# The passages into and out of W_up in a hybrid encoder layer: split order, product order, and the order of loads, sums and stores

## The chip, the cores and the metric

The kernel runs on one core of a Trainium2 chip. The core has five engines with an instruction stream each: PE (matrix products, with PEld for its weight loads), DVE (VectorE), ACT (ScalarE), POOL (GpSimd) and SP (SyncE, which here issues every DMA). They wait for each other through semaphores. The metric is the device time of one execution in microseconds (us); lower is better. Three runs of the kernel before took 1406.53, 1408.93 and 1409.12 us, median 1408.93.

## The reference

One layer of a streaming encoder on 1024 prompt rows and 64 sample rows of width 1024: an input projection, three kinds of mixing (forgetting attention, a gated unit, stick-breaking attention), an output projection, a layer norm, and then the part that matters here:

```
def sq_relu_mlp(x, w_up, w_down):
    h = jnp.square(jax.nn.relu(jnp.einsum('btd,df->btf', x, w_up)))
    return jnp.einsum('btf,fd->btd', h, w_down)

xp = layer_norm(ALPHA * xp + sq_relu_mlp(xp, w_up[l], w_down[l]), ln2_g[l], ln2_b[l])
```

W_up is 1024 by 4096 and W_down 4096 by 1024, all in float32; the sample rows go through the same layer.

## The kernel before, in words

Every float32 product is made from three passes in a faster format: each operand is split into a high part (a copy by ScalarE) and a low part (a subtraction, line 97, by VectorE or POOL), and high times high, high times low and low times high are added up. In place of 8 block products of a 2 by 2 blocking, the kernel computes 7 (a Strassen-like scheme), which needs sums and differences of the operands beforehand and of the results behind.

**W_up ("up", from about 690 to 1040 us).** The columns of W_up are taken in 16 pairs p of 256 columns. The rows are two token groups: s=0 with 288 columns of the products (the samples' 32 among them) and s=1 with 256. `Chain(p, s)` (L1253) holds one pair and one group: `product(i)` (L1260) is 12 matmuls at L1272 into PSUM banks named zA to zD, each followed by an evacuation (a ScalarE copy L1283 for A, VectorE sums L1286 to L1292); `relu` (L1304) makes the squared relu of the eight results in place, `sums` (L1313 to L1316) the four combinations that W_down's 7 products want, and stores them to DRAM: `h4_dr` (L1317), `h3_dr` (L1318) and for s=0 the sample columns `hs_dr` (L1321). The weights of a pair arrive by `up_load` (L1463), tile wr, are split into wa (L1212 and L97) and summed and split into ws.

The token operand comes from rows that a layer norm has just finished. `x_steps` (L1140) is a generator: for the rows of pair nm ("0" and "1" are s=0, "2" and "3" are s=1) it transposes four blocks on PE into PSUM tiles xtb, xta, xtd and xtc (tag pt, two buffers, so that the third transposition waits for what reads the first), copies and splits them into the operands xo, and forms the four combinations tt[0] to tt[3] (L1168, L1172, then L1174 or L1181, then L1182) with splits of their own. Between its steps the first products are issued by hand.

**W_down ("down", from about 1040 us on).** W_down is taken in 16 groups g of 256 of its rows, two (c = g // 2) sharing a set of split weights wd; group g multiplies the h of pairs p. `wd_load` (L1386) brings weights into rd (for the second half of the first set: into awa, the buffer that held the last wa), `wd_sum` (L1404) and `wd_split` form and split the combinations. `h_load` (L1421) reads stored h back (into hx, hr and awa), `h_split` makes its high part on ScalarE (L1431), copies that to a PSUM tile st (L1435) and subtracts on VectorE (L1436). The first h of group 0, tile h4a, is loaded by four DMAs (L1628). `Down.product` (L1730) is 6 matmuls and `evac` adds the result to accumulators (L1695, L1697), which `acc_load` (L1447, L1450) first fills with the layer's input. `first_group` (L1852) does group 0 by hand; `hs_load` and `b12_again` (L1849) belong to the samples' product (L1774, L1776), which comes behind group 0.

**What sets the order.** SP issues DMAs in program order, and each waits for the eighth before it. Inside `in_order(...)` (L99) each engine's stream is pinned to the order in which the code is written; that holds for the first up pair, the borders p=1 and from p=14, and `first_group`. Only the pairs between and the later groups are placed by the scheduler. In the last part of up, c2 is pair 14 with s=0, c3 is pair 15 with s=1, and c4 is pair 15 with s=0; c0 and c1 at the start are the first pair's chains.

Of the kernel before, what the change touches and what calls it, by code (L numbers as in the profile page):

```python
# [12 lines left out]
F32 = mybir.dt.float32  # L13
# [7 lines left out]
P = 128  # L21
PASSES = ((0, 0), (0, 1), (1, 0))
D = 1024
# [4 lines left out]
NB = TP // P  # L28
# [28 lines left out]
def _build(nc, tc, a, es):  # L57
# [1082 lines left out]
    def x_steps(nm, s, c0, n, r0, n0, r1, n1):  # L1140
# [32 lines left out]
        if s == 0:  # L1173
            nc.vector.tensor_tensor(tt[:, 2], p22, c12, op=ALU.subtract)  # L1174
# [3 lines left out]
        if s == 1:  # L1178

            split_t(4, nc.vector)  # L1180
            nc.vector.tensor_tensor(tt[:, 2], p22, c12, op=ALU.subtract)  # L1181
        nc.vector.tensor_tensor(tt[:, 3], tt[:, 1], p21, op=ALU.subtract)  # L1182
        yield
        if s == 0:
            hi = xo0[:, 3:7, :, 0, cs]
            nc.scalar.activation(hi.rearrange("p o k c -> p (o k) c"), tt.rearrange("p o k c -> p (o k) c"), AF.Copy)
            lo_sub(nc.vector, xo0[:, 3:7, :, 1, cs].rearrange("p o k c -> p (o k) c"),
                   tt.rearrange("p o k c -> p (o k) c"), hi.rearrange("p o k c -> p (o k) c"))
        else:
            for o in (3, 5, 6):  # L1190
                split_t(o, nc.vector if o < 5 or nm == "3" else nc.gpsimd)
# [132 lines left out]
    for i in range(MIXED, NT):  # L1324
        t = ORD[i]
# [132 lines left out]
    with p3:  # L1458
# [51 lines left out]
        t = ORD[-1]  # L1510
        next(x2)
        with in_order(border):
# [39 lines left out]
            low()  # L1552
            c0.finish()
            c1.product(6)
# [44 lines left out]
        def products(c, some):  # L1599
            for i in some:  # L1600
                c.product(i, False)

        with in_order(border):
# [19 lines left out]

            h4 = lp.tile([P, 2, 2, 2, 4, P], F32R, name="h4a", tag="ws")
            hbuf[0, 0], hbuf[0, 1] = h4[:, 0], h4[:, 1]
            for q in range(2):
                for x in range(2):
                    nc.sync.dma_start(h4[:, x, 1, q].bitcast(F32), h4_dr[q, 0][:, :, x * P:(x + 1) * P])  # L1628
            awa = lp.tile([P, 3, D], F32, name="awa", tag="wa")
            hx = lp.tile([P, D], F32, name="hx", tag="hx")  # L1630
# [4 lines left out]
            h_load(0, 1, 0)  # L1635
            wd_load(0, 1, awa[:, 0:2].rearrange("p q (o c) -> p (q o) c", o=2))
            products(c3, (1,))
            c2.relu()
            products(c3, (2,))
            c2.sums()  # L1640
            acc_load(0)
            products(c3, (3, 4))
            h_split(0, 0, 0, ("o", "s"))
            products(c3, (5, 6))
            c4 = chain(NP - 1, 0)
# [6 lines left out]
            def both_pairs(n):  # L1652
                for q in range(2):
                    wd_split(0, q, n, nc.gpsimd)

            both_pairs(0)
            products(c4, (1,))
            h_split(0, 0, 1, ("o", "s"))
            both_pairs(2)
            for q in range(2):  # L1660
                wd_sum(0, q, 0, nc.vector)
            products(c4, (2,))
            both_pairs(1)
            wd_sum(0, 0, 1, nc.vector)
            products(c4, (3, 4))
            wd_sum(0, 1, 1, nc.vector)
            products(c4, (5,))
            h_load(0, 1, 1)
            for q in range(2):
                wd_sum(0, q, 2, nc.vector)  # L1670
            h_split(0, 1, 0, ("tr", "s"))
            both_pairs(3)
            products(c4, (6,))
            both_pairs(4)
    xst.close()


    with ExitStack() as p3:
# [173 lines left out]
        def first_group():  # L1852
# [10 lines left out]
            for q in range(2):  # L1863
                wd_sum(0, q, 3, nc.vector)
# [5 lines left out]
            both(1)  # L1870
            for q in range(2):
                wd_split(0, q, 6, nc.gpsimd)
            for q in range(2):
                h_load(1, 1, q)
            both(2)
            h_split(1, 0, 0, None, (0,))
            c4.relu()
# [3 lines left out]
            c3.relu()  # L1881
            both(4)
            h_split(1, 0, 0, None, (1,))
            c3.sums(nc.gpsimd)
            c4.sums()
            h_split(1, 0, 1)
            both(5)
            a37 = lp.tile([P, 2, D], F32, name="acc37", tag="hh1")
            two(3, a37[:, 0])
            two(7, a37[:, 1])  # L1890
            for t in (2, 6, 3, 7, NB):
                acc_load(t)
# [15 lines left out]
        for c in range(NC - 1):  # L1908
            for part in range(2):
# [3 lines left out]
                if g == 1:  # L1913
                    hs_load(0)
                    for q in range(2):
                        b12_again(0, q)
# [191 lines left out]
```

## Time and profile before

| what | value |
|---|---|
| median of three runs | 1408.93 us |
| profiled execution, own time | 1403.64 us |
| its span, first to last instruction | 1401.8 us |
| mean granted TensorE clock | 0.984 |
| PE busy | 1323.6 us, 94% |
| VectorE, ScalarE, POOL busy | 996.3, 720.1, 608.5 us |
| DMA traffic | 168.87 MB, mean 120 GB/s |

Times in the timelines are microseconds from the span's start. A row gives start, duration, engine, line, operation, output<-inputs and count; the bracket at its end holds how long the engine had been idle before it and whose instruction released it. In rows of windows each engine has its busy time and, in round brackets, its number of instructions; the granted clock is 1.00 at full speed. SPq rows are the issue of a DMA, not its transfer; the DMA view gives the time from issue to landing.

### The profile page before, as it was taken

The numbers are of one execution on the slowest core, as the hardware profiler recorded it, in microseconds if no ns is written. First come the engines' busy times: TensorE is split into PE (matmuls) and PEld (weight loads), VectorE is DVE, ScalarE is ACT, GpSimd is POOL, SyncE is SP. The second block draws the span as 40 slices with busy tenths as digits, with TensorE's granted clock in tenths as the row PEclk, the third lists the DMA queues.
The fourth block names the chain that finished last, engine by engine and source line by source line (L and its number), as shares of the span: only waits on it lengthen the run. The fifth ranks groups of instructions, "written<-read, shape, count | busy, mean of one in ns | idle before, by whom it ended". The sixth has DMA issues, their size and how long they took to land.

```text
span 1401.8 us, 24289 instructions
## 1 busy us (share of the span) xinstructions
PE 1323.6 (94%) x8827; PEld 1205.5 (86%) x8827; DVE 996.3 (71%) x1795; ACT 720.1 (51%) x1561; POOL 608.5 (43%) x667
## 2 busy tenths in 40 slices
PE   7899999999989997999899999999998999999996
PEld 6899999999888986866789999999986788887874
DVE  3566566677787499787776677687668677667677
ACT  3366565666565476333432332322256677667665
POOL 3222232356565445755421222122156765555647
PEclk9999999999999998999999999999999999999998
DMA  7334242321313434432223444443468244344343
GB/s 219 72 84 113 58 113 66 83 59 49 95 27 80 115 97 130 143 112 68 76 85 113 160 152 131 153 141 127 162 223 316 90 169 138 130 153 146 106 135 128
DMA packets 150257, 168.87 MB, mean 120 GB/s; under 512 B 27116, under 2 KB 116524, under 8 KB 150136
## 3 DMA queue, kind: packets, MB, share of 16 engines
q1 hardware_dynamic: 150136, 167.30, 38.1%
q8 instruction: 70, 1.15, 0.3%
q14 instruction: 51, 0.42, 0.1%
HBM read 109.26 MB, written 51.71 MB: 115 GB/s over the span
## 4 chain that ended last, share of the span: by engine, by line
PE 54%; DVE 13%; DMA 10%; POOL 8%; ACT 8%; issue 5%; SPq 1%; DVEq 0%; ACTq 0%; POOLq 0%
PE zA L1272 9%; PE zD L1272 6%; PE mx L244 5%; PE kvsb L355 5%; PE kvfox L355 4%; POOL wd L97 3%; DMA rd<-w_down 3%; PE zC L1272 3%; PE zB L1272 3%; DMA awa<-h_dr 2%; POOL rd L1404 2%; PE qfox L496 2%; PE Sfox L554 2%; ACT wd L1212 2%; PE ptfox L602 1%
## 5 line engine op out<-in xcount | busy, mean ns | idle before, releaser
L97 POOL TENSOR_TENSOR wa<-wr,wa 128x512 fp32r<-128x512 f32 x42 | 63.6, 1544 | 225.3 <-ACT wa L1212 203.8
L97 POOL TENSOR_TENSOR wd<-rd,wd 128x512 fp32r<-128x512 f32 x77 | 100.5, 1317 | 108.0 <-ACT wd L1212 94.8
L244 PE MATMUL mx<-xT,oTb 128*128 128x512 f32 (+1 forms) x416 | 105.6, 405 | 1.6 <-ACT oTb L202 1.5
L1272 PE MATMUL zD<-xo,ws 128*128 128x288 f32 (+1 forms) x720 | 98.1, 289 | 3.1 <-DVE h4a L1436 2.7
L1272 PE MATMUL zA<-xo,ws 128*128 128x288 f32 (+1 forms) x720 | 98.2, 290 | 0.0
L1272 PEld LDWEIGHTS zD<-xo,ws 128*128 128x128 f32 x720 | 93.7, 189 | 3.6 <-DVE h4a L1436 2.9
L244 PEld LDWEIGHTS mx<-xT,oTb 128*128 128x128 f32 (+1 forms) x416 | 76.3, 189 | 21.1 <-ACT oTb L202 2.5
L1272 PEld LDWEIGHTS zA<-xo,ws 128*128 128x128 f32 x720 | 94.3, 190 | 0.0
L355 PE MATMUL kvfox<-wkvfox,xT 128*128 128x256 f32 (+3 forms) x624 | 90.8, 294 | 2.4 <-DVE fx L458 1.3
L540 POOL TENSOR_TENSOR sgsb<-sgsb,snsb 128x127 f32<-128x127 f32 (+7 forms) x48 | 58.9, 1228 | 78.7 <-DVE snsb L538 64.3
L1404 POOL TENSOR_TENSOR rd<-rd 128x512 f32<-128x512 f32 x56 | 79.4, 1419 | 30.4 <-DVE b L97 28.1
L355 PE MATMUL kvsb<-wkvsb,xT 128*128 128x256 f32 (+1 forms) x624 | 87.7, 286 | 0.0
L1212 ACT ACTIVATE wd<-rd 128x512 fp32r<-128x512 f32 x105 | 63.4, 623 | 44.2 <-POOL rd L1404 21.9
L1730 PE MATMUL A<-wd,wd 128*128 128x512 f32 x312 | 83.3, 396 | 3.0 <-DVE acc L1697 2.0
L355 PEld LDWEIGHTS kvfox<-wkvfox,xT 128*128 128x128 f32 (+1 forms) x624 | 81.9, 194 | 4.1 <-DVE fx L458 1.6
L538 DVE TENSOR_TENSOR_SCAN snsb<-snsb,one 128x128 f32<-128x128 f32 (+7 forms) x48 | 72.3, 1509 | 13.3 <-ACT snsb L537 12.7
L355 PEld LDWEIGHTS kvsb<-wkvsb,xT 128*128 128x128 f32 (+1 forms) x624 | 79.3, 187 | 0.2
L1283 ACT ACTIVATE sn<-zA 128x256 f32<-128x256 f32 (+1 forms) x80 | 31.0, 390 | 92.2 <-PE zA L1272 77.5
L1730 PEld LDWEIGHTS A<-wd,wd 128*128 128x128 f32 x312 | 58.0, 188 | 19.1 <-DVE acc L1697 3.5
L1730 PE MATMUL A<-wd,h4a 128*128 128x512 f32 x240 | 64.2, 393 | 1.2 <-DVE acc L1697 0.7
L1490 ACT ACTIVATE ws<-wr 128x1024 fp32r<-128x1024 f32 x28 | 29.0, 1057 | 56.9 <-DVE wr L1222 56.9
L1730 PEld LDWEIGHTS A<-wd,h4a 128*128 128x128 f32 x240 | 44.8, 188 | 12.3 <-ACT wd L1212 1.1
(548 smaller groups left out, 3750.5 us busy)
## 6 DMA issues: line engine op xcount, KB each, us to landing
h_dr<-hh SPq DMA_DIRECT2D x30, 512.0 KB, 3.2
rd<-w_down SPq DMA_DIRECT2D x30, 512.0 KB, 4.4
wr<-w_up SPq DMA_DIRECT2D x13, 1024.0 KB, 5.5
hr<-h_dr SPq DMA_DIRECT2D x31, 384.0 KB, 3.8
h_dr<-hh SPq DMA_DIRECT2D x30, 384.0 KB, 4.0
raw<-w_in SPq DMA_DIRECT2D x44, 256.0 KB, 3.4
hx<-h_dr SPq DMA_DIRECT2D x15, 512.0 KB, 3.8
awa<-h_dr SPq DMA_DIRECT2D x15, 512.0 KB, 4.1
```

The source lines that it names most:

```text
L97: eng.tensor_tensor(out, src, hi.bitcast(F32), op=ALU.subtract)
L244: nc.tensor.matmul(acc[0:m], oT[:, k, hx, 0:m], wo[k // 4][hw][:, k % 4, cs], start=(i == 0), stop=(i == len(seq) - 1))
L355: nc.tensor.matmul(acc[0:n, c0:c0 + n1 - n0], xT[k // 4][:, k % 4, c:c + n], wt[:, k, hw, n0:n1], start=(i == 0), stop=(i == len(seq) - 1))
L496: nc.tensor.matmul(acc[:, 0:w], wq[:, k, hw, :], xT[k // 4][:, k % 4, c:c + w], start=(i == 0), stop=(i == len(seq) - 1))
L538: nc.vector.tensor_tensor_scan(g[:, 0:n][:, ::-1], g[:, 0:n][:, ::-1], one.broadcast_to([P, n]), 1.0, op0=ALU.mult, op1=ALU.bypass)
L540: nc.gpsimd.tensor_tensor(s[:, 0:n - 1], s[:, 0:n - 1], g[:, 1:n], op=ALU.mult)
L1212: nc.scalar.activation(hi, raw, AF.Copy)
L1272: nc.tensor.matmul(z, w[:, hw, k], xop(s, bo, hx)[:, k, :], start=(new and k == 0 and j == 0), stop=(k == 3 and j == 2), skip_group_check= ...
L1283: nc.scalar.activation(c, z, AF.Copy)
L1404: eng.tensor_tensor(r[:, o], r[:, x], r[:, y], op=ALU.subtract)
L1490: nc.scalar.activation(ws[:, 0, q, c], src[:, q], AF.Copy)
L1730: nc.tensor.matmul(z, h[:, hx, q, o], wset[self.c % 2][q][:, hw, wb], start=((n in (0, 3) or n == 1 and self.c == 0) and q == 0 and j == 0 ...
```

## The change

It touches four places and removes no arithmetic. (1) In `x_steps` the early split of operand 4 and the late tt[2] now happen only for pair "3"; pair "2" forms tt[2] at L1174, and splits operand 4 at the end. (2) In the first pair, c1's last product comes ahead of `c0.finish()`, so c1's evacuation, relu, sums and stores stand ahead of c0's on VectorE and SP. (3) In the last pair of up, c2's relu, sums and stores come ahead of the load of W_down's second half into awa; both h_splits of h4a come ahead of c3's products 1 and 3; the loads of hx and the second h3 piece, the accumulator load and wd's sums change place; c3's relu and sums (on VectorE instead of POOL) move up from `first_group`, wd's fourth sum to the end of up. (4) In `first_group`, c4's relu and sums, the accumulator loads of tiles 3, 7 (buffer hh1) and 2, 6 (hh0) move up, and hs_load and b12_again come in from group 1.

```diff
@@ x_steps
         nc.vector.tensor_tensor(tt[:, 1], p22, tt[:, 0], op=ALU.subtract)
-        if s == 0:
+        if nm != "3":
             nc.vector.tensor_tensor(tt[:, 2], p22, c12, op=ALU.subtract)
         yield
         p21 = tr(r0, 1, n0, "c")
         both(1, p21)
-        if s == 1:
+        if nm == "3":
 
             split_t(4, nc.vector)
             nc.vector.tensor_tensor(tt[:, 2], p22, c12, op=ALU.subtract)
...
-            for o in (3, 5, 6):
+            for o in (3, 5, 6) if nm == "3" else (4, 3, 5, 6):
                 split_t(o, nc.vector if o < 5 or nm == "3" else nc.gpsimd)
@@ first pair
             low()
+            c1.product(6)
             c0.finish()
-            c1.product(6)
@@ last pair of up
                     nc.sync.dma_start(h4[:, x, 1, q].bitcast(F32), h4_dr[q, 0][:, :, x * P:(x + 1) * P])
+            hx = lp.tile([P, D], F32, name="hx", tag="hx")
+            h_load(0, 1, 0)
             awa = lp.tile([P, 3, D], F32, name="awa", tag="wa")
-            hx = lp.tile([P, D], F32, name="hx", tag="hx")
...
-            h_load(0, 1, 0)
+            c2.relu()
+            c2.sums()
             wd_load(0, 1, awa[:, 0:2].rearrange("p q (o c) -> p (q o) c", o=2))
-            products(c3, (1,))
-            c2.relu()
-            products(c3, (2,))
-            c2.sums()
+            h_split(0, 0, 0, ("o", "s"))
+            products(c3, (1, 2))
+            h_split(0, 0, 1, ("o", "s"))
+            products(c3, (3, 4))
             acc_load(0)
-            products(c3, (3, 4))
-            h_split(0, 0, 0, ("o", "s"))
             products(c3, (5, 6))
+            h_load(0, 1, 1)
             c4 = chain(NP - 1, 0)
             products(c4, (0,))
...
             both_pairs(0)
+            c3.relu()
+            c3.sums()
             products(c4, (1,))
-            h_split(0, 0, 1, ("o", "s"))
             both_pairs(2)
+            products(c4, (2,))
+            both_pairs(1)
             for q in range(2):
                 wd_sum(0, q, 0, nc.vector)
-            products(c4, (2,))
-            both_pairs(1)
-            wd_sum(0, 0, 1, nc.vector)
             products(c4, (3, 4))
-            wd_sum(0, 1, 1, nc.vector)
+            h_split(0, 1, 0, ("tr", "s"))
+            for q in range(2):
+                wd_sum(0, q, 1, nc.vector)
             products(c4, (5,))
-            h_load(0, 1, 1)
             for q in range(2):
                 wd_sum(0, q, 2, nc.vector)
-            h_split(0, 1, 0, ("tr", "s"))
             both_pairs(3)
             products(c4, (6,))
             both_pairs(4)
+            for q in range(2):
+                wd_sum(0, q, 3, nc.vector)
@@ first_group
-            for q in range(2):
-                wd_sum(0, q, 3, nc.vector)
             both(0)
...
             both(1)
+            c4.relu()
...
             both(2)
+            c4.sums()
             h_split(1, 0, 0, None, (0,))
-            c4.relu()
+            a37 = lp.tile([P, 2, D], F32, name="acc37", tag="hh1")
+            two(3, a37[:, 0])
+            two(7, a37[:, 1])
+            for t in (3, 7):
+                acc_load(t)
             both(3)
             h_load(1, 0, 1)
             wd_load(1, 0)
-            c3.relu()
+            for t in (2, 6, NB):
+                acc_load(t)
             both(4)
             h_split(1, 0, 0, None, (1,))
-            c3.sums(nc.gpsimd)
-            c4.sums()
             h_split(1, 0, 1)
+            hs_load(0)
+            for q in range(2):
+                b12_again(0, q)
             both(5)
-            a37 = lp.tile([P, 2, D], F32, name="acc37", tag="hh1")
-            two(3, a37[:, 0])
-            two(7, a37[:, 1])
-            for t in (2, 6, 3, 7, NB):
-                acc_load(t)
@@ the loop over groups
-                if g == 1:
-                    hs_load(0)
-                    for q in range(2):
-                        b12_again(0, q)
                 wd_load(c + 1, part)
```

## The prediction

> **What bounds the kernel now.** The page first, then the windows, then engine by engine the timelines of two stretches, the start of W_up (685 to 735 us) and the passage into W_down (1014 to 1090 us), because the diff touches nothing else.
>
> ```profile
> span 1401.8 us, 24289 instructions
> PE 1323.6 (94%) x8827; PEld 1205.5 (86%) x8827; DVE 996.3 (71%) x1795; ACT 720.1 (51%) x1561; POOL 608.5 (43%) x667
> ```
>
> TensorE is busy 94% of the span, and no product is added or removed. All the change can move is PE's idle time at the two borders, plus the time its clock is down. PE's timeline at the first border (start, duration, instruction, and in brackets idle time and releaser):
>
> ```profile
> 694.69 1.02 PE L1148 MATMUL xtb<-ident,y 128*128 128x128 f32 x4 [3.36 <-DVE xr L1181]
> 695.36 3.10 PE L1272 MATMUL zA<-xo,oTb 128*128 128x288 f32 x12
> ...
> 698.66 1.84 PE L1272 MATMUL zC<-xo,w 128*128 128x288 f32 x12
> 701.00 0.63 PE L1148 MATMUL xtd<-ident,y 128*128 128x128 f32 x4 [0.50 <-DVE xr L1168]
> ...
> 730.57 0.40 PE L1272 MATMUL zA<-xo,wa 128*128 128x288 f32 x1 [1.18 <-ACT wa L1212]
> 731.93 2.71 PE L1272 MATMUL zA<-xo,wa 128*128 128x288 f32 x11 [0.96 <-POOL wa L97]
> ```
>
> And at the second border:
>
> ```profile
> 1021.87 1.59 PE L1272 MATMUL zA<-xo,ws 128*128 128x256 f32 x12
> ...
> 1033.73 1.88 PE L1272 MATMUL zD<-xo,ws 128*128 128x288 f32 x12 [2.67 <-DVE h4a L1436]
> ...
> 1039.25 1.89 PE L1272 MATMUL zD<-xo,ws 128*128 128x288 f32 x12 [0.46 <-DVE hh L1286]
> 1040.97 2.89 PE L1730 MATMUL A<-wd,h4a 128*128 128x512 f32 x12
> ...
> 1064.04 1.67 PE L1730 MATMUL D<-wd,h4b 128*128 128x512 f32 x6
> ...
> 1073.46 0.98 PE L1730 MATMUL A<-wd 128*128 128x512 f32 x3 [0.87 <-DVE acc L1695]
> ...
> 1075.88 0.94 PE L1730 MATMUL A<-wd,h4a 128*128 128x512 f32 x3 [0.74 <-DVE acc L1697]
> 1077.86 0.96 PE L1730 MATMUL D<-wd 128*128 128x512 f32 x3 [1.04 <-DVE acc L1695]
> ...
> 1080.25 0.96 PE L1730 MATMUL A<-wd,wd 128*128 128x512 f32 x3 [0.75 <-DVE acc L1695]
> ...
> 1087.24 0.40 PE L1774 MATMUL ds<-wd,hs 128*128 128x512 f32 x1
> ```
>
> The brackets are the prize: 3.36, 0.50 and 2.14 us at the first border, 2.67, 0.46 and 3.40 (0.87, 0.74, 1.04 and 0.75) at the second. Some of it also costs clock. The first window follows the 2.14 us of waits at W_up's first new weights; the second holds the 2.67 us gap. After the busy times of PE, PEld, DVE, ACT and POOL the row has the granted clock:
>
> ```profile
> 733.00:735.00 2.00, 2.00 (x10) 2.00 (x10) 1.97 (x2) 0.27 (x1) 2.00 (x2) 0.50 0.00 0
> 1030.00:1040.00 10.00, 6.88 (x50) 6.41 (x49) 7.37 (x9) 6.36 (x13) 7.40 (x6) 1.00 0.18 68
> ```
>
> **First border, x_steps.** For pair "2", L1174's subtraction goes ahead, so xtd's PSUM buffer is free without waiting for L1181, and the early split of operand 4 goes to the end. VectorE's rows:
>
> ```profile
> 689.80 2.38 DVE L150 TENSOR_TENSOR y<-y,gb 128x512 f32<-128x512 f32 x2 [1.25 <-POOL y L143]
> ...
> 693.86 0.68 DVE L1181 TENSOR_TENSOR xr<-xtd,c 128x512 f32<-128x512 f32 x1
> ```
>
> The subtraction (0.68) fits into the 1.25 idle ahead of L150. So xtb starts when L150's first half is done, about 691.2, and the 3.36 goes; so does the slow clock behind it (3.10 against 1.84, 1.02 against 0.6: 1.6 in all) and the 0.50. In their place come PE's waits for the next late things, estimated from the order of the rows: about 0.6 for xta (L1182), 0.8 for zC (ScalarE's copy) and 0.5 for xtd. 3.36 + 1.6 + 0.5 - 1.9 = 3.6 us earlier at the products behind.
>
> **First border, the last product ahead of the sums.** This reorders VectorE and SP: the s=1 chain's evacuation, sums and two stores come first, the s=0 chain's with its three hs stores last, right before the load of the next weights.
>
> ```profile
> 720.30 1.28 DVE L1304 SCALAR_TENSOR_TENSOR y<-y 128x512 f32<-128x512 f32 x2
> ...
> 723.21 0.45 DVE L1288 TENSOR_TENSOR hh<-zB,sn 128x288 f32<-128x288 f32 x1
> ```
> ```profile
> 720.65 2.31 SPq L1321 DMA_DIRECT2D hs_dr<-h  x3
> ...
> 724.08 1.77 SPq L1463 DMA_DIRECT2D wr<-w_up  x2
> ```
>
> VectorE's total is unchanged, so the sums still end near 723.4. But now 2.31 us of hs stores stand between their end and the load: 726.4 instead of 724.08, and 3.6 earlier by the step above: the load is 1.3 us earlier in all. PE stands 3.6 earlier, so its wait at 730.57 grows by 2.3, and the border gains **1.3 us**. Bounds: a gain of 3.6 if the load's wait has cover that I don't see, a loss of 1.0 if the longer gap costs as much clock again as the 2.71 row (11 matmuls at 1.84/12 each would be 1.69).
>
> **Second border, h_split of the first group ahead of c3's products.** ScalarE's rows:
>
> ```profile
> 1020.66 0.39 ACT L1283 ACTIVATE sn<-zA 128x256 f32<-128x256 f32 x1 [2.41 <-PE zA L1272]
> ...
> 1023.78 0.62 ACT L1431 ACTIVATE h4a<-h4a 128x512 fp32r<-128x512 f32 x1
> 1024.43 0.60 ACT L1435 ACTIVATE st<-h4a 128x512 f32<-128x512 f32 x1
> ```
> ```profile
> 1016.44 2.79 SPq L1628 DMA_DIRECT2D h4a<-h_dr  x4
> ...
> 1053.41 0.33 SPq L1421 DMA_DIRECT2D awa<-h_dr  x1
> ...
> 1059.84 0.33 SPq L1317 DMA_DIRECT2D h_dr<-hh  x1
> ```
> ```profile
> h4a<-h_dr SPq DMA_DIRECT2D x2, 256.0 KB, 4.0
> ```
> ```profile
> h4a<-h_dr SPq DMA_DIRECT2D x2, 256.0 KB, 6.1
> ```
>
> The first two of the four h4a loads took 4.0 us to land, the last two 6.1. The third is issued near 1017.8 and lands near 1023.9. In the changed order four ScalarE instructions that need loads one and three stand ahead of the 0.39 us copy at 1020.66, which frees zA for the product that began at 1021.87. ScalarE does the last two (0.62 + 0.60) from 1023.9, then the copy: about 1025.5, and PE waits **3.6 us** where it waited for nothing. Had the third load taken 4.0, it would be 1.5. Against this the 2.67 and the 0.46 go. The 2.67 was VectorE's: its L1288 waited on the hs store, which now is ahead of the 1 MB of awa loads:
>
> ```profile
> 1032.63 0.46 DVE L1288 TENSOR_TENSOR hh<-zB,sn 128x288 f32<-128x288 f32 x1 [5.02 <-DMA hs_dr<-hh]
> ```
>
> With 0.2 of small waits W_down starts 0.7 later than 1040.97 (3.6 + 0.2 - 2.67 - 0.46). If no load blocks ScalarE it is 3.1 earlier; if the gap costs the clock, another 1.0 to 1.6 later. W_down's second half behind the h stores costs nothing itself: its first sums start at 1034 and later.
>
> **Second border, the sums and the h loads of the first groups.** The third set of wd sums now stands behind h_split(0,1,0), some 3 us later on VectorE and POOL, and hx comes free later:
>
> ```profile
> 1046.52 0.55 DVE L1436 TENSOR_TENSOR wd<-hx,st 128x384 fp32r<-128x384 f32 x1 [1.46 <-ACT st L1435]
> ```
> ```profile
> 1050.96 0.63 ACT L1431 ACTIVATE h4b<-hx 128x512 fp32r<-128x512 f32 x1 [2.43 <-DMA hx<-h_dr]
> ...
> 1057.54 0.63 ACT L1431 ACTIVATE h4b<-awa 128x512 fp32r<-128x512 f32 x1 [2.56 <-DMA awa<-h_dr]
> ```
>
> 1046.52 becomes about 1049.25, so hx lands near 1053.7 instead of 1050.9 and the first h4b product waits near 1.8; c4's relu, now ahead of the evacuations, adds most of the rest: PE stands 4.2 late around 1058.
>
> ```profile
> 1053.47 1.35 DVE L1304 SCALAR_TENSOR_TENSOR hh<-hh 128x1152 f32<-128x1152 f32 x1
> ```
>
> Next, SP: c4's stores and the acc37 loads now stand ahead of the load of h4b's second half. That load was issued at 1053.41 and used at 1057.54. Now it waits for c4's sums (some 1058), follows their stores and the acc37 loads, about 1061, and has some 5 us to land: 1066.3. The product of 1064.04 then starts at about 1071.3, **7.3 late** (all since 1021.87, not to be added to the 0.7 and 4.2). From there the 3.40 us of waits on accumulators goes, since their loads and the evacuations now lead: 3.9 late at 1087.24. POOL leaves c3's sums (four instructions) but gets hs and b12_again ahead of the splits of W_down's next group, which came at 1062.67 before; I take 2.0 for that, between 0 (hidden by the time that PE is late itself) and 4 (one of the three splits, 3.83 / 3, too late for each of three products).
>
> ```profile
> 1062.67 3.83 POOL L97 TENSOR_TENSOR wd<-rd,wd 128x512 fp32r<-128x512 f32 x3
> ```
>
> The border loses **5.9 us**; bounds are a gain of 3 (neither transfer blocks) and a loss of 10.
>
> The sum: -1.3 + 5.9 = +4.6 us. The profiled execution's own time was 1403.64, so it would take 1408.2; the median of the runs shown is 1408.93, 5.3 above, so **1413.5**.
>
> **The clock.** The rows: 3.36 idle was followed by 3.10 for 1.84 of work, 2.67 by 1.88 and a clock of 1.00, and 0.40 of work between 1.18 and 0.96 by a clock of 0.50. So a gap of the length of my 3.6 can cost up to 1.6 more, and its cost depends on more than its length. The Trainium skill (TensorE: Matmul & The Clock Gate, Part 1: The HAM clock gate) says that the array's clock is halved by activity seen in free-running windows of about 3.4 us. By that rule a 3.6 us gap would be punished or not depending on where the windows lie; the 2.14 us gap that drew 0.50 agrees only if a window mostly idle is enough.
>
> **The rivals.** First, slower still: both new gaps (3.6 at 1021.87, 4.4 at 730) cost the clock, 1.6 and 1.0, and the next W_down loads cost 4 rather than 2: 4.6 + 4.6 gives 1418. For it: the 3.36 gap did; against it: the 2.67 did not. Second, faster: the load of h4b's second half is in time. Then nothing is added behind W_down's start (+0.7), the accumulators' waits still go (-3.40), and with the first border's -1.3 it is -4.0: 1405. It decides if that load is issued before about 1056, that is if c4's sums end by 1054. Against it: on VectorE they stand behind the evacuations of the third pair of products, which use h4b and are late themselves. Third, no change: h4a's third load lands as fast as the first (4.0, so 2.1 less) and h4b's second half about 2.5 earlier, so that the sum is 0: 1409.
>
> **Chances.** Forecast 0.43, slower still 0.20, faster 0.24, no change 0.13. A measurement here can tell about 0.2%, 2.8 us. Slower holds 0.63, within 0.12, faster 0.25. The range from 1403.5 to 1420 takes in all four with about half of their tails; the likeliest case's own range is 1409.5 to 1417.
>
> **What would show it.** Right: no wait at xtb near 691; a wait of 4 us or more at W_up's first new weights; PE idle near 1022 released by ScalarE's copy; no wait on L1436 in c4's first products; a wait at D<-wd,h4b released by L1431 on an awa load; no waits on acc behind. Wrong: PE busy through 1022, or h4b's second half landing before PE asks for it.

## The result, and the profile after

The changed kernel took 1419.26 us in the median of four runs (1415.22 to 1422.24), against 1407.73 for the kernel before beside it: ratio 1.0103, 95% interval 1.008 to 1.0126 (the two medians alone give 1.0082). In another series with six runs of it the median was 1415.34 against 1403.89, the ratio 1.0083 (1.0066 to 1.0099). So it is 11.5 us slower by the medians of either series and 12 to 14.5 by the ratios; the forecast was 4.6 us slower. The time lies in the stated range, at its upper end, the direction is right, and the size is about a third to two fifths of what was measured. The profiled execution spans 1420.5 us, 18.7 more than before's, but it is the slowest of its four, and before's profiled execution (1403.64) is faster than the four beside it, so this pair of traces shows more than the medians do. The profiled execution of the second series (below "the changed kernel again") spans 1413.0, 11.2 more. Of all the executions behind this document one took twice as long, 2872.04 us, in the first run with hs in group 1; the ratio of that run leaves it out.

PE's timeline of the changed kernel at the first border:

```profile
692.77 0.63 PE L1148 MATMUL xtb<-ident,y 128*128 128x128 f32 x4 [0.38 <-DVE y L150]
693.16 1.83 PE L1272 MATMUL zA<-xo,oTb 128*128 128x288 f32 x12
...
728.87 0.40 PE L1272 MATMUL zA<-xo,wa 128*128 128x288 f32 x1 [2.12 <-ACT wa L1212]
730.21 3.01 PE L1272 MATMUL zA<-xo,wa 128*128 128x288 f32 x11 [0.95 <-POOL wa L97]
```

The 3.36 us ahead of xtb are 0.38 and the slow products behind it are gone; the wait for W_up's new weights grew from 1.18 to 2.12. At the second border (lines of the down part are two higher than before):

```profile
1023.00 2.62 PE L1272 MATMUL zA<-xo,ws 128*128 128x256 f32 x12 [2.82 <-ACT sn L1283]
1025.42 2.22 PE L1272 MATMUL zC<-xo,wa 128*128 128x256 f32 x12
...
1040.25 2.93 PE L1732 MATMUL A<-wd,h4a 128*128 128x512 f32 x12
...
1052.92 0.73 PE L1732 MATMUL A<-wd,h4b 128*128 128x512 f32 x2 [1.41 <-ACT h4b L1431]
1055.85 1.65 PE L1732 MATMUL A<-wd 128*128 128x512 f32 x3 [2.21 <-DVE awa L1697]
...
1069.05 0.74 PE L1732 MATMUL A<-wd,h4b 128*128 128x512 f32 x2 [2.14 <-ACT h4b L1431]
...
1073.46 2.11 PE L1732 MATMUL D<-wd,h4b 128*128 128x512 f32 x6
...
1099.46 0.50 PE L1732 MATMUL A<-wd,h4a 128*128 128x512 f32 x1 [0.62 <-ACT wd L1212]
1100.81 0.74 PE L1732 MATMUL A<-wd,h4a 128*128 128x512 f32 x2 [0.62 <-POOL wd L97]
```

Every wait that the prediction named for this border is there, and the waits of 2.67 us and of 3.40 us (four on acc) are gone. ScalarE's and SP's rows behind two of them:

```profile
1021.38 0.63 ACT L1431 ACTIVATE h4a<-h4a 128x512 fp32r<-128x512 f32 x1 [1.70 <-DMA h4a<-h_dr]
1022.05 0.60 ACT L1435 ACTIVATE st<-h4a 128x512 f32<-128x512 f32 x1
1022.58 0.37 ACT L1283 ACTIVATE sn<-zA 128x256 f32<-128x256 f32 x1
```
```profile
1060.37 1.15 SPq L1447 DMA_DIRECT2D acc<-x_dr  x2
1061.63 0.38 SPq L1421 DMA_DIRECT2D awa<-h_dr  x1
```

The copy that frees zA stands behind the wait for h4a's third load. The load of h4b's second half is issued at 1061.63, behind c4's stores and the acc37 loads (before: 1053.41).

**Where the time went, in equal work.** The product order differs from the first group on, so rows can't be set side by side. But from W_down's first product to the end each trace has the same 1472 matmul records of one length. The table has, for the n-th of them, its start less that in the profiled execution of before, less the same difference at the product ahead of the first border (zD at 689.56 before, 690.63 after). It shows what each kernel gained (-) or lost (+), in us, from the first border up to that work; "predicted" is the forecast's sum up to there.

| n-th matmul (its start before) | 0 (1041) | 72 (1058) | 96 (1064) | 168 (1085) | 288 (1113) | 1200 (1324) | last |
|---|---|---|---|---|---|---|---|
| predicted | -0.6 | +2.9 | +6.0 | +2.6 | +4.6 | +4.6 | +4.6 |
| changed kernel | -1.8 | +4.7 | +8.4 | +5.5 | +9.1 | +17.8 | +17.5 |
| changed kernel again | -3.9 | +1.8 | +5.2 | +1.8 | +5.3 | +10.7 | +10.7 |

W_down starts earlier than forecast in both executions of the changed kernel. From the 72nd to the 168th matmul, the end of what the forecast argued about the first group, the two bracket it; then both lose 3.5 where it had 2.0, and then 8.7 and 5.4 in the groups behind, where it had nothing. The difference between the two up to there is in good part the clock: its missing share in these windows makes 6.8 us in the first (0.17, 0.29, 0.05 and 0.17 of ten each) and 3.4 in the second (0, 0.17, 0.15 and 0.02), some of it while PE was idle.

```profile
1020.00:1030.00 10.00, 7.18 (x47) 7.00 (x46) 4.53 (x9) 4.18 (x8) 0.00 (x0) 0.83 0.84 299
1050.00:1060.00 10.00, 6.39 (x19) 4.50 (x18) 9.72 (x15) 1.23 (x2) 7.28 (x5) 0.71 0.48 177
1060.00:1070.00 10.00, 7.65 (x31) 5.64 (x29) 1.41 (x3) 3.70 (x7) 0.00 (x0) 0.95 0.98 342
1070.00:1080.00 10.00, 9.37 (x33) 7.05 (x34) 7.35 (x13) 6.56 (x15) 3.09 (x4) 0.83 0.99 301
```

The same view of the changed kernel again:

```profile
1020.00:1030.00 10.00, 8.52 (x66) 8.33 (x67) 6.63 (x11) 5.75 (x13) 1.07 (x1) 1.00 0.96 327
1050.00:1060.00 10.00, 7.68 (x25) 5.89 (x26) 8.10 (x14) 0.64 (x2) 4.49 (x3) 0.83 0.46 140
1060.00:1070.00 10.00, 7.43 (x25) 4.84 (x24) 3.22 (x6) 6.54 (x12) 0.00 (x0) 0.85 1.03 375
1070.00:1080.00 10.00, 10.00 (x44) 8.07 (x43) 7.62 (x13) 7.91 (x17) 7.50 (x7) 0.98 0.86 289
```

What the later groups lose shows in PE's waits between 1115 and 1335 us (total, times, longest). Before has none in that stretch; the changed kernel has nine of 0.20 to 0.63, 3.2 us in all:

```profile
PE A L1732 <- ACT p L1749: 1.2, 3, 0.6
PE B L1732 <- ACT B L1720: 0.7, 3, 0.3
PE A L1732 <- POOL wd L97: 0.6, 1, 0.6
PE A L1732 <- DVE acc L1699: 0.4, 1, 0.4
PE A L1732 <- DVE awa L1699: 0.3, 1, 0.3
```

Beside them many matmuls start some 0.1 us late: behind the hundredth, 45 steps from one to the next are 0.3 to 0.4 us long, against 13 in before, where 0.23 is usual. The edit does not name these groups. But the scheduler, not the code's order, places the instructions of groups 1 to 13, and its result changed: of the 890 matmuls from the 300th on, 405 have other operands than before's at the same place.

### The profile page after: what moved, and what is told of

Read it like the earlier page. It is cut to its first block, busy times and chain, and to the rows that moved or that the text cites. A ratio compares the mean times of both kernels' runs of the same rounds, so it can differ in the third digit from the quotient of the medians.

```text
span 1420.5 us, 24276 instructions
## 1 busy us (share of the span) xinstructions
PE 1336.6 (94%) x8827; PEld 1208.3 (85%) x8827; DVE 1005.5 (71%) x1799; ACT 720.8 (51%) x1561; POOL 605.7 (43%) x663
## 4 chain that ended last, share of the span: by engine, by line
PE 53%; DVE 12%; POOL 10%; DMA 9%; ACT 8%; issue 6%; SPq 1%; DVEq 0%; POOLq 0%; ACTq 0%
PE zA L1272 9%; PE zD L1272 6%; PE kvsb L355 5%; PE mx L244 5%; PE kvfox L355 4%; DMA rd<-w_down 4%; POOL wd L97 4%; PE zC L1272 3%; PE zB L1272 3%; POOL rd L1404 3%; PE qfox L496 2%; PE Sfox L554 2%; DVE snsb L538 2%; PE qsb L496 1%; ACT wd L1212 1%
## 5 line engine op out<-in xcount | busy, mean ns | idle before, releaser
L97 POOL TENSOR_TENSOR wa<-wr,wa 128x512 fp32r<-128x512 f32 x42 | 62.4, 1512 | 227.4 <-ACT wa L1212 213.8
L97 POOL TENSOR_TENSOR wd<-rd,wd 128x512 fp32r<-128x512 f32 x77 | 103.0, 1351 | 116.6 <-ACT wd L1212 116.6
L1212 ACT ACTIVATE wd<-rd 128x512 fp32r<-128x512 f32 x105 | 63.7, 624 | 66.6 <-POOL rd L1404 32.5
L1732 PE MATMUL A<-wd,wd 128*128 128x512 f32 x312 | 85.2, 402 | 1.9 <-DVE acc L1699 1.5
L1732 PEld LDWEIGHTS A<-wd,wd 128*128 128x128 f32 x312 | 58.8, 191 | 18.8 <-DVE acc L1699 3.7
L1732 PE MATMUL A<-wd,h4a 128*128 128x512 f32 x240 | 67.2, 404 | 4.6 <-POOL wd L97 1.3
L1732 PEld LDWEIGHTS A<-wd,h4a 128*128 128x128 f32 x240 | 44.5, 190 | 20.1 <-ACT p L1749 2.5
```

What stands on the lines that cost most here:

```text
L97: eng.tensor_tensor(out, src, hi.bitcast(F32), op=ALU.subtract)
L1212: nc.scalar.activation(hi, raw, AF.Copy)
L1732: nc.tensor.matmul(z, h[:, hx, q, o], wset[self.c % 2][q][:, hw, wb], start=((n in (0, 3) or n == 1 and self.c == 0) and q == 0 and j == 0 ...
```

## The experiments

Ratios are to the kernel before, run on the same chip. The 95% intervals stand in brackets; the table at the end of this section has the traces.

**The start of W_up.** First x_steps' change alone, then with the product moved ahead of the sums:

```diff
-        if s == 0:
+        if nm != "3":
             nc.vector.tensor_tensor(tt[:, 2], p22, c12, op=ALU.subtract)
...
-        if s == 1:
+        if nm == "3":
 
             split_t(4, nc.vector)
...
-            for o in (3, 5, 6):
+            for o in (3, 5, 6) if nm == "3" else (4, 3, 5, 6):
```

```diff
+            c1.product(6)
             c0.finish()
-            c1.product(6)
```

> The kernel before with the change to x_steps alone (pair 2 forms tt[2] early). The prediction's first step: no 3.36 us wait at the xtb transposition, products behind it 3.6 us earlier, and, since the stores keep their order, the load of W_up's third pair also issued 3.6 us earlier: PE's wait for it unchanged, 3.6 us gained, ratio 0.997. Rival: the load's wait has no part in it (PE idle is only moved to the new weights): about 0, ratio 1.000.

> The kernel before with both changes at the start of W_up, nothing at the end. The prediction: 1.3 us gained (load issued 1.3 us earlier). In the changed kernel's trace this border came out 2.9 us earlier; so 1.3 to 2.9 us faster, ratio 0.998 to 0.999, and 1 to 2.5 us slower than with x_steps' change alone. Rival: the order of products and sums is free, then as fast as x_steps' change alone.

Measured 0.998 (0.9962 to 0.9997) and 0.9987 (0.9971 to 1.0003). PE in the run with x_steps' change alone, and SP in the same run:

```profile
691.53 0.63 PE L1148 MATMUL xtb<-ident,y 128*128 128x128 f32 x4 [0.40 <-DVE y L150]
...
726.67 0.40 PE L1272 MATMUL zA<-xo,wa 128*128 128x288 f32 x1 [1.14 <-ACT wa L1212]
```
```profile
720.24 1.78 SPq L1463 DMA_DIRECT2D wr<-w_up  x2
```

The load goes out 3.84 us earlier than before's 724.08 (3.67 counted from zD of the same trace) and PE's wait for it stays (1.14 against 1.18): the gain is whole, as expected. With both edits it goes out at 722.12, and PE's wait is 2.11. So in the traces the moved product takes back part of the gain; by the intervals the two kernels can't be told apart.

**The splits of h4a behind the products.**

```diff
-            h_split(0, 0, 0, ("o", "s"))
             products(c3, (1, 2))
-            h_split(0, 0, 1, ("o", "s"))
             products(c3, (3, 4))
+            h_split(0, 0, 0, ("o", "s"))
+            h_split(0, 0, 1, ("o", "s"))
```

> The changed kernel with both h_splits of h4a put back behind c3's products 1 to 4. If ScalarE's wait for h4a's third load is what stops PE at product 4, the 2.82 us idle and the slow clock behind it go: W_down starts about 4 us earlier than in the changed kernel, and the whole is 3 to 4.5 us faster than it (ratio to before about 1.007). Rival: the h4b load and the order in the later groups set the end anyway, then as slow as the changed kernel, ratio 1.010.

Measured 1.0082 (1.0054 to 1.0109), not told apart from the changed kernel. Product 4 waits for nothing, so the cause of that stall is confirmed; but another came, at c4's last product:

```profile
1033.56 3.25 PE L1272 MATMUL zD<-xo,ws 128*128 128x288 f32 x12 [4.48 <-DVE hh L1286]
```

VectorE was late there because c3's four sums took 1.4 us each in place of 0.42, while POOL ran its splits back to back (VectorE's first sum and POOL's split beside it):

```profile
1025.18 1.40 DVE L1313 TENSOR_TENSOR hh<-hh 128x256 f32<-128x256 f32 x1
```
```profile
1026.26 1.47 POOL L97 TENSOR_TENSOR wd<-rd,wd 128x512 fp32r<-128x512 f32 x1
```

The changed kernel has the same inside one run of sums: the first two took 0.43 each, and the other two 1.56 and 1.50, once POOL's splits had begun at 1031.71. The Trainium skill (SBUF — State Buffer, SBUF: two separate sides) says that a VectorE operation with two SBUF inputs and a GpSimd operation that reads SBUF take a shared port pair as an exclusive lock, so that one waits for the whole instruction of the other; the trace agrees, as the short sum takes as long as the long split. So undoing this edit alone gained little: c3's early sums filled the place.

**The first group as before**, the borders as changed (c3's relu and sums and wd's fourth sum stay early):

```diff
             both(1)
-            c4.relu()
...
             both(2)
-            c4.sums()
             h_split(1, 0, 0, None, (0,))
+            c4.relu()
...
             h_split(1, 0, 0, None, (1,))
+            c4.sums()
             h_split(1, 0, 1)
-            hs_load(0)
...
             both(5)
+            a37 = lp.tile([P, 2, D], F32, name="acc37", tag="hh1")
+            two(3, a37[:, 0])
+            two(7, a37[:, 1])
+            for t in (2, 6, 3, 7, NB):
+                acc_load(t)
```

> The changed kernel with the first group of W_down as before (c4's relu, sums, stores and the accumulator loads at their old places, hs_load and b12_again in group 1), c3's sums and wd's fourth sum staying early. If c4's stores and the acc37 loads ahead of h4b's second load cost what the trace shows (D<-wd,h4b 9 us late), that wait goes and before's 3.4 us on accumulators come back: 4 to 8 us faster than the changed kernel, ratio to before 1.005 to 1.008, and no wait of the placed groups after 1110 us. Rival: the placed groups are late for their new order, whatever the first group does: waits on p, B and acc stay after 1110, ratio 1.009 or more.

Measured 1.0038 (1.0022 to 1.0055): by the ratio faster than either theory had it. At the 288th matmul it is 2.0 us ahead of before, with the stall at product 4 still in it. Then it loses 6.9 to the end, though PE enters these groups early. That raised the question of their order.

**The order of the later groups.** In the next runs the instructions of groups 1 to 13 are chained, engine by engine, in a given order:

```python
for e, o in GROUPS.items():          # o: the order wanted, for engine e
    for x, y in zip(o, o[1:]):
        tc.add_manual_dep(by[e][y], by[e][x].name, mybir.DependencyInfo(
            mybir.DependencyClass.NoSync, mybir.DependencyReason.DATA), reason="groups")
```

In the profiles of the chained kernels the lines stand 72 or 73 higher: L1284 and L1285 are L1212, L170 is L97, L1804 is L1732, L1821 is L1749.

> The changed kernel, in which the instructions of the groups behind the first (g = 1 to 13) are put by hand into the order, engine by engine, that the scheduler gave them in the kernel before. If the 8 us that are lost between 1100 and 1340 us come from that order, the small waits of PE there go and the whole is about 8 us faster than the changed kernel: ratio to before 1.004 to 1.006. Rival: PE loses them because weights, splits and accumulators are late from the first group on, whatever the order: ratio 1.009 or more, waits on p, B and acc unchanged.

> The kernel before with nothing changed but the order of the groups behind the first: it is the one that the scheduler gave them in the run with the old first group. If the order alone costs, about 7 us slower than before (ratio 1.005) with small waits of PE between 1180 and 1350 us. Rival, lateness from the border: ratio 1.000.

The kernel before with the other order, the one that the scheduler gave the run with the old first group: 1.0039 (1.0026 to 1.0051). The order alone costs, and it costs with both borders untouched. (It is not the chaining: a kernel chained in before's order took 0.9989, further down.) Its trace loses 5 us from the 288th to the 1200th matmul. But in the changed kernel the old order gained nothing: 1.0094 (1.0074 to 1.0115). So it was run again with the changed kernel beside it:

> The changed kernel once more, beside the next three: ratio to before 1.009 to 1.012.

> The changed kernel with the later groups in before's order once more, now on the same chip as the changed kernel. If the order costs what the two traces show, 4 us faster than the changed kernel (ratio to before lower by 0.003). Rival, lateness alone: the same within 0.1%.

1.0083 (1.0066 to 1.0099) and 1.0099 (1.0082 to 1.0115): putting back before's order does not win the loss back. In the trace that order pays 7.9 us between the 168th and 288th matmul (6.6 in the run before it), and nothing in the groups behind. Its largest wait there, with the clock at half for 6.83 us from 1100.41, which is up to 3.4 of the 7.9:

```profile
1100.87 0.80 PE L1804 MATMUL D<-wd,h4a 128*128 128x512 f32 x1 [2.88 <-ACT wd L1284]
```

**The load of h4b's second half first**, the groups in before's order:

```diff
             both(2)
-            c4.sums()
             h_split(1, 0, 0, None, (0,))
-            a37 = lp.tile([P, 2, D], F32, name="acc37", tag="hh1")
-            two(3, a37[:, 0])
-            two(7, a37[:, 1])
-            for t in (3, 7):
-                acc_load(t)
             both(3)
             h_load(1, 0, 1)
+            c4.sums()
+            a37 = lp.tile([P, 2, D], F32, name="acc37", tag="hh1")
+            two(3, a37[:, 0])
+            two(7, a37[:, 1])
+            for t in (3, 7):
+                acc_load(t)
```

> As the run with the groups as before, and c4's sums, their stores and the loads of accumulators 3 and 7 put behind the load of h4b's second half. If that load's place on SP's queue is what makes D<-wd,h4b late, PE's 2.1 us wait for L1431 and the half clock behind it go and the run is 4 to 7 us faster than the one with the groups as before. Rival: the accumulators' waits of before (3.4 us) come back or the first h4b wait (2.21 on awa L1697) is the one that matters: within 2 us of it.

Measured 1.0094 (1.0071 to 1.0116), no gain. The load's place does what was said: it goes out at 1052.96 and the 96th matmul comes 4.0 us sooner than in the run it is compared with (+2.6 against +6.6). But the next wait takes it all back:

```profile
1076.98 2.93 PE L1804 MATMUL A<-wd,h4b 128*128 128x512 f32 x6 [7.95 <-ACT p L1821]
```
```profile
1072.87 0.51 ACT L1284 ACTIVATE hs<-acc 128x128 fp32r<-128x128 f32 x2 [8.46 <-DMA acc<-hs_dr]
```

ScalarE stood for 8.46 us at the splits of hs, whose two loads of 64 KB took 10.1 us to land behind loads of accumulators and weights, and the copy of p that frees a PSUM bank stood behind it. In the changed kernel the same load has POOL standing:

```profile
1076.72 0.89 POOL L97 TENSOR_TENSOR hs<-acc,hs 128x128 fp32r<-128x128 f32 x2 [19.39 <-ACT hs L1212]
...
1080.33 4.71 POOL L97 TENSOR_TENSOR wd<-rd,wd 128x512 fp32r<-128x512 f32 x3
```

```profile
acc<-hs_dr SPq DMA_DIRECT2D x2, 64.0 KB, 10.5
```

POOL idles 19.39 us and starts W_down's next splits at 1080.33 (before: 1062.67). Not all of that is the wait for hs: the next weights, issued at 1062.05, took 7.6 us to land.

**hs_load and b12_again back in group 1**, all else as changed, the groups in before's order. It was run twice; the trace read is that of the second:

```diff
             h_split(1, 0, 1)
-            hs_load(0)
-            for q in range(2):
-                b12_again(0, q)
             both(5)
...
+                if g == 1:
+                    hs_load(0)
+                    for q in range(2):
+                        b12_again(0, q)
                 wd_load(c + 1, part)
```

> The changed kernel with hs_load and b12_again put back into group 1, the later groups in before's order. If POOL's 19 us of idleness ahead of hs (it waits for the sample columns' load) is what makes W_down's next splits late, the 6.6 us that PE loses between 1088 and 1115 us go: 4 to 7 us faster than the run with the groups as before, ratio to before 1.004 to 1.006. Rival: the splits are late for the late h4b and rd loads ahead of them, then within 2 us of it, ratio 1.009.

> The changed kernel with hs_load and b12_again in group 1 and the later groups in before's order, once more, for its trace. If POOL's wait ahead of hs is the cause, POOL starts the splits of W_down's next set some 15 us sooner (about 1065 in place of 1080), PE has no wait on wd between 1088 and 1115, and what is left against before stays at what the h4b load cost, 3 to 6 us. Rival: the waits on wd stay and the ratio of 1.005 has another cause.

Measured 1.0048 (1.0032 to 1.0063) and 1.0071 (1.0045 to 1.0096), against 1.0094 and 1.0099 with hs early. In the trace the 7.9 us between the 168th and 288th matmul are 0.0. POOL's splits come at 1073.00, less early than the 1065 that was expected. They wait for ScalarE's copies of rd, which stand right behind its splits of the late h4b and h4a; the two rd loads, issued from 1063.58 on, had landed after 6.8 us in the median:

```profile
1072.31 1.65 ACT L1285 ACTIVATE wd<-rd 128x512 fp32r<-128x512 f32 x3
```
```profile
1073.00 3.80 POOL L170 TENSOR_TENSOR wd<-rd,wd 128x512 fp32r<-128x512 f32 x3 [11.35 <-ACT wd L1285]
```

So hs_load and b12_again ahead of these splits hold POOL some 7 us longer (to 1080.33 in the changed kernel, 1073.00 here), and by the ratios they cost 3 to 7 us with this order. With the scheduler's own order:

> The same with the later groups in the order that the scheduler gives them. If that order costs by itself, as in the kernel before with other groups, 5 to 7 us slower than the run above: ratio to before 1.009 to 1.010, with PE's small waits spread from 1180 to 1340. If only lateness costs: the same as the run above, 1.005.

1.0078 (1.0058 to 1.0098): not told apart from 1.0071. The traces show two ways to the same end. The scheduler's order is 6.8 us better up to the 168th matmul (+1.2 against +8.0), and pays 7.6 from the 288th to the 1200th, where before's order pays 0.2. Of the 7.6, 2.70 are one wait for a split of wd, ahead of 1304.17, with half clock for 3.41 us from 1303.99. And where nothing is late:

> The run with the old first group, the later groups in before's order. Its trace was 2.6 us ahead of before at 1090 us and lost 6.9 us from 1200 on. If the order did that, the 2.6 us stay: ratio to before 0.998 to 0.999. If not: 1.004 as it was.

0.9989 (0.9972 to 1.0006), against 1.0038 in the scheduler's order. PE's waits between 1115 and 1335 us are none with before's order and these with the scheduler's:

```profile
PE A L1732 <- ACT wd L1212: 1.7, 2, 0.9
PE D L1732 <- DVE acc L1699: 1.2, 1, 1.2
PE A L1732 <- DVE wd L1436: 0.5, 1, 0.5
PE A L1732 <- DVE acc L1699: 0.3, 1, 0.3
PE B L1732 <- ACT B L1720: 0.2, 1, 0.2
```

**The parts that help together:** x_steps' change, c2's sums ahead of the awa load and c3's sums early; before's order elsewhere, in the first of the two runs with wd's sums, the load of the second h3 piece and its split in the changed order. Beside x_steps' change, and acc_load(0) behind the first h_split, the second run differs from before by this:

```diff
+            h_load(0, 1, 0)
             awa = lp.tile([P, 3, D], F32, name="awa", tag="wa")
...
+            c2.relu()
+            c2.sums()
             wd_load(0, 1, awa[:, 0:2].rearrange("p q (o c) -> p (q o) c", o=2))
...
             both_pairs(0)
+            c3.relu()
+            c3.sums()
             products(c4, (1,))
             h_split(0, 0, 1, ("o", "s"))
...
             both(3)
             h_load(1, 0, 1)
             wd_load(1, 0)
-            c3.relu()
...
-            c3.sums(nc.gpsimd)
```

> x_steps' change (products and sums of the first pair in the old order), c2's sums ahead of the awa load, c3's sums early, both h_splits of h4a and the first group's stores and loads as before, the later groups in before's order. By the readings so far: 4 us at the first border, no stall at product 4, no h4b wait, 3.4 us of accumulator waits gone: 7 to 10 us faster than before, ratio 0.993 to 0.995. Rival: the waits come back elsewhere at the second border (as the 4.48 us in the run with late splits) and it ends like x_steps' change alone, ratio 0.998.

> Only what has paid: x_steps' change, c2's sums ahead of the awa load, c3's relu and sums early; everything else, the order of the later groups too, as before. Expected: the 1.3 us wait for the first h4b load of the run with the parts that help goes, so 1 us better than that one: 7 us faster than before, ratio 0.995. Rival: W_down's start is then as in x_steps' change alone, ratio 0.997 to 0.998.

Measured 0.997 (0.9954 to 0.9986) and 0.9967 (0.9954 to 0.9981), 1398.76 us in the median for the second. Both beat both kernels and both miss what was expected: most of what is gained is x_steps' change, and the second border's parts end, by these intervals, as the rival had it.

The traces of the runs, in the table's measure of the first section:

| kernel | 0 | 72 | 96 | 168 | 288 | 1200 | last |
|---|---|---|---|---|---|---|---|
| x_steps alone | -5.0 | -4.2 | -4.2 | -5.6 | -5.4 | -5.9 | -5.7 |
| both edits of the first border | -4.0 | -3.2 | -3.3 | -3.2 | -3.2 | -3.7 | -2.2 |
| splits of h4a late | -0.6 | +2.8 | +7.7 | +4.6 | +7.6 | +13.6 | +13.1 |
| old first group | -0.9 | +3.2 | +2.3 | -2.0 | -2.0 | +3.5 | +4.9 |
| old first group, before's order | -2.4 | +0.2 | -0.7 | -2.9 | -2.8 | -3.3 | -1.7 |
| before, other order | -1.5 | -0.7 | -0.7 | +0.2 | +0.2 | +5.2 | +6.8 |
| changed, before's order | -2.5 | +4.3 | +6.6 | +6.6 | +13.2 | +12.8 | +14.2 |
| the same again | -2.0 | +3.7 | +7.2 | +7.9 | +15.8 | +15.3 | +17.4 |
| and h4b's load first | -2.1 | +3.5 | +2.6 | +9.1 | +13.2 | +12.8 | +14.1 |
| hs in group 1, before's order | -1.1 | +5.5 | +7.9 | +8.0 | +8.0 | +8.2 | +9.8 |
| hs in group 1, own order | -2.8 | +4.2 | +5.8 | +1.2 | +2.8 | +10.5 | +10.2 |
| parts that help | -5.4 | -2.7 | -3.4 | -5.2 | -5.2 | -5.7 | -5.1 |
| two parts | -4.2 | -3.4 | -4.2 | -6.1 | -5.9 | -6.3 | -3.7 |

The row "before, other order" has the kernel before's own borders, so its -1.5 at W_down's start is what one execution differs from another; differences of that size are not read here.

From the 288th to the 1200th matmul the rows of this table and of the first fall into two sets. Where PE's matmuls stand in before's order (nine rows; with x_steps alone and with both edits of the first border the scheduler itself chose it), they go from -0.5 to +0.2, also where PE enters that stretch 8.0 to 15.8 us late. Where they stand in an order that the scheduler chose behind a changed second border (the other four and the changed kernel's two), they lose 5.0 to 8.7, also where PE enters 2.0 early or on time. So the loss in that stretch belongs to the order. What before's order costs with hs early stands ahead of it, between the 168th and the 288th.

## Why the prediction was right or wrong

- **x_steps: right.** The wait went, the new small waits came (0.43 and 0.34, where 0.8 and 0.5 were estimated; 0.38 stayed at xtb, and the 0.6 at xta did not come), and zD came at 699.21 in place of 701.82, counted from 690.63 and 689.56: 3.7 us earlier, 3.6 forecast.
- **The last product ahead of the sums: right in its place and direction.** The load at 723.76 is 1.4 us earlier in that count, 1.3 forecast. PE's wait grew by only 0.94, not 2.3, since the data came sooner behind the issue: the product that needs them followed it by 5.1 us, in before by 6.5. So the border gained 2.8 us at that product (728.87 against 730.57, in that count), not 1.3, and the sign "a wait of 4 us or more" failed: the two waits are 2.12 and 0.95.
- **ScalarE's wait for h4a's third load: right.** 2.82 us of wait where 3.6 was forecast, 1.68 in the second trace, since the load took 5.5 and 4.3 us to land in place of 6.1. W_down's start, -0.6 forecast, came at -1.8 and -3.9. The clock price that was kept as a bound was paid in one of the two executions (2.62 and 2.22 for two products of 1.59 and 1.58).
- **The first group's h loads: two places of three right, and the total is partly luck.** hx was not late: its load was issued at 1048.52 against 1047.10, 0.35 us later in that count (1.7 earlier in the second trace), where 2.7 was forecast. The wait at the first h4b product is there because PE came early: up to there 1.8 and 1.7 us of W_down's early start are given back.

```profile
1047.10 0.32 SPq L1421 DMA_DIRECT2D hx<-h_dr  x1
```
```profile
1048.52 0.32 SPq L1421 DMA_DIRECT2D hx<-h_dr  x1
```

The first row is before's, the second the changed kernel's. c4's relu ahead of the evacuations cost a wait of 2.21 us (0.68 with the relu back, in the old first group), and the half clock came behind it; so the stretch from W_down's start to the 72nd matmul lost 6.4 and 5.7 where 3.5 was forecast, and only W_down's earlier start brought +8.4 and +5.2 at the 96th matmul near the +6.0 that was forecast. From the 72nd to the 96th, where h4b's second half is late, 3.1 was forecast and 3.7 and 3.4 measured. The accumulators' 3.40 us did go.
- **W_down's next weights: the term was too small.** 2.0 forecast, 3.5 measured in both traces. The step looked only at POOL's work; what held POOL beyond the late weights was its wait for hs, whose loads of 64 KB land behind the accumulators'. With hs back the loss goes to 0.0 in before's order and 1.6 in the scheduler's.
- **"The diff touches nothing else": this step failed.** The forecast compared instruction orders only for the borders. The scheduler placed groups 1 to 13 anew behind the changed border, and their loss, 8.7 and 5.4 us in the two traces, is the larger part of what was missed; the forecast had put it at nothing. That the order has a price of its own is shown twice without lateness (1.0039 for the order alone; 1.0038 against 0.9989), and in the changed kernel before's order removes the loss behind the 288th matmul (-0.5 in both traces). But it pays about as much more ahead of it, between the 168th and the 288th (6.6 and 7.9 against 3.5), so the whole is no faster. Why the new order's matmuls start late one by one, and whether a third order would avoid both losses, stays open.
- **The rivals.** The rival "slower still", 1418, came closest to the time, but not by its reasons: the next loads cost 3.5 of its 4, the clock did cost at the second border, but the greater part came from the later groups, which it did not name. The faster rival's condition, h4b's load in time, was not met: c4's sums ended near 1058. Where the load was made early the gain went into the hs wait. The third, no change, had one condition nearly met in the second trace (h4a's third load landed in 4.3 us, 4.0 asked), and that kernel was slower all the same by the later groups' loss, which no rival had.

## What to carry to other kernels

Where a scheduler places a loop, an edit right ahead of the loop can change the loop (here every edit at the second border did that was not chained, and the edits at the first border, 300 us ahead, did not): compare its order on every engine and give it a term of its own. Here that alone was worth 0.4 to 0.5%. A copy or a small load that is moved "sooner" carries its wait with it, and the engines that run in order stand behind it: ask what is queued behind each moved wait, down to the 64 KB load in a full queue. And put differences on equal work, not on equal rows, once the order differs.

## What the runs showed of the hardware

- The granted clock falls to half in stretches of 3.41 us or a multiple of it (6.83, and 10.24 in three traces) in the clock records of all these traces, but for the one at the kernel's end. Whether a gap of 1.3 to 3 us draws one differs between executions of one program: after the stall at product 4 the clock was 0.83 in one trace of the changed kernel (a wait of 2.82 us) and 1.00 in the other (1.68). Within a trace the stretches begin whole multiples of 3.413 us apart: in the changed kernel's at 729.86, 1023.40, 1054.12 and 1071.19, with 86, 9 and 5 times 3.413 between them. The Trainium skill (TensorE: Matmul & The Clock Gate, Part 1: The HAM clock gate) gives a free-running window of 3413 ns; the length agrees, and so does this grid.
- On that grid the price of a gap can be read off. In the 16 traces, between 600 and 1385 us, every window at full clock in which PE was busy for less than 47% was followed by half clock (43 of 43), and none in which it was busy for 52% or more (0 of 3512); in between it was 23 of 28. So the place of a gap in the grid counts beside its length. The changed kernel's stall at product 4 left PE 0.59 us of one window (the first row, with the half clock in the second); before's 2.67 us gap was shared out between two windows (the other rows):

```profile
1019.99:1023.40 3.41, 0.59 (x5) 0.40 (x4) 1.14 (x3) 1.98 (x4) 0.00 (x0) 1.00 0.99 342
1023.40:1026.81 3.41, 3.41 (x18) 3.41 (x18) 2.11 (x4) 2.20 (x5) 0.00 (x0) 0.50 1.04 358
```
```profile
1029.28:1032.69 3.41, 1.79 (x14) 1.55 (x12) 0.06 (x1) 3.35 (x7) 2.54 (x3) 1.00 0.74 275
1032.69:1036.11 3.42, 2.38 (x17) 2.38 (x18) 3.42 (x5) 1.44 (x4) 3.42 (x3) 1.00 0.03 11
```

- The 128x256 sum took 0.42 us alone and 1.40 beside POOL's splits.
- Two loads of 64 KB took 10.5 us to land behind five accumulator loads, h4b's second half and two loads of W_down in the same queue. Later in the same kernel, between 1086 and 1112 us, two took 1.8:

```profile
acc<-hs_dr SPq DMA_DIRECT2D x2, 64.0 KB, 1.8
```
